# Zero-padded low parts of q, masks as planned units, and casts that the planner may give to ScalarE or VectorE, in a hybrid SSD and attention layer

## The chip, the core and the metric

The kernel runs as one program on one core of a Trainium2 chip. The metric is the device time of one execution in microseconds (us). The kernel before ran three times: 936.17, 939.4 and 940.26 us, median 939.4. One more execution was profiled; it took 935.09 us, and the profile's span, from its first to its last instruction, is 933.4 us.

## The reference

A decoder layer on 512 tokens of width 1024, in float32. In short:

```
h1  = rms_norm(x) * (1 + scale1) + shift1            # scale, shift, gate from silu(c) @ w_ada
z, xbc, dt, q, k, v = split(h1 @ w_in)
y_ssd = group_norm( (SSD scan of xbc, 16 heads, 4 chunks of 128) * silu(z) )
q, k  = rms_norm per head of 64 (q also / 8)
for (window, dilation) in (128,1), (512,4), (2048,16):
    softmax attention over t, t-d, t-2d, ...; the three are merged by their softmax denominators
y_att = rms_norm(merged)
x = x + gate1 * (concat(y_ssd, y_att) @ w_out)
x = x + gate2 * (square(relu(h2 @ w_ff1)) @ w_ff2)    # h2: a second modulated rms_norm
```

The three dilated windows are computed as one causal softmax whose scores get an additive mask: 0, log 2 or log 3 where one, two or three windows hold the key, and -1e30 where none does.

## The kernel before, in words

Activations lie transposed, with channels on the 128 partitions and the 512 tokens along the free dimension. Each float32 operand of a product is split into a high part (a cast to the type fp32r) and a low part (the operand less that cast). A dense product is three matmuls, high by high, high by low and low by high (`mm3`, lines 149 to 152). A weight tile (128 x 1024) comes by DMA into `wraw`, ScalarE casts the high part `whi`, GpSimd or VectorE subtracts the low part `wlo`, and 24 matmuls of 128 x 512 use it.

The stages in order of time: norm 1 and the first projections (to about 90 us); the convolution channels (`conv`, lines 560 to 586), each with one ScalarE and three VectorE passes (line 568) out of the PSUM bank; then a long region in which a planner decides the order (to about 560 us); then the last part of the output projection, norm 2 and the MLP to the end, in which dense products follow one another.

Just before the region, in iteration `n == 8` of the loop at line 945, `make_masks()` (lines 406 to 441) is called. It builds the attention mask and four small selection matrices (`selm`, `gsum`, `selT`, `gsel`) and clears `rhl`, with iota and affine selects on GpSimd and everything else on VectorE.

The region holds the z, q, k and v projections (the jobs of line 182, eight tiles of z, then four batches of q, k and v), the SSD scan of 16 heads, the gated norm, the attention of 16 heads in eight pairs, and most of the output projection. Each step is a unit: an engine, a cost in ns, the function that issues it, what it needs and makes, the buffers that it takes and gives back, and a due time (`unit`, line 1022). `place_units` (lines 1025 to 1089) goes through them by list scheduling: on each engine the unit that can start first, with a slack in favour of the one due earlier; the engine with the earliest start issues next. It assumes the written costs, and VectorE free from 8000 ns on. The order found is the program order of every engine and of the DMA queue on SyncE (SP); at run time each engine works in that order and waits at semaphores.

In the SSD scan each head needs VectorE for a product with the decay (line 676), for a low part of 128 x 1280 (line 684) and for two additions of a result (lines 694 and 696). Attention may open only when all 16 heads are summed (`att_open`, line 1279), as it reuses their memory.

For each q or k tile a square is taken on ScalarE, its high part is cast on VectorE (`sq_hi`, line 742), its low part is subtracted on GpSimd (`sq_lo`), and two matmuls sum rows (lines 1188 and 1189). The four gated-norm groups go the same way.

For the scores of a pair of heads, `st_dma` stacks tiles: QA holds the high part of q of the even head twice, once on each half of the partitions; KA holds the high part of k of that head above and its low part below; QB and KB serve the odd head. One matmul of 128 rows then gives high by high plus high by low. The low part of q, made by GpSimd for both heads in one tile `ql` of which there are two (`st_lo`, lines 797 to 802), needs only the high part of k, so its matmul uses 64 rows:

```
nc.tensor.matmul(p[:, o:o + w], lhsT=ql[r, s], rhs=Ks[r, :w], start=False, stop=True)
```

Each head has four such couples, of 512, 384, 128 and 256 columns (lines 843 to 850). Then VectorE adds the mask and takes the maximum (line 859), ScalarE exponentiates (`soft`), VectorE divides by the sums in four passes (`att_norm`, lines 872 to 877), TensorE transposes (line 887), ScalarE and VectorE make high and low parts (lines 894 and 900), and eight matmuls weigh v (`weighted_sum`, line 623; the SSD heads use it too).

The second half of the modulation vector is computed by 32 steps on VectorE (`ada_step`, line 1004, helper line 278) that read tiles by DMA.

Of the kernel before, what the change touches and what calls it, by code (L numbers as in the profile page):

```python
# [10 lines left out]
F32 = mybir.dt.float32  # L11
# [6 lines left out]
P = 128  # L18
T = 512
# [25 lines left out]
def tile_hybrid_layer(ctx, tc, xT, vec, c_row, ada_e, ada_r, w_a, w_dt, w_x, w_z, w_v, w_qk,  # L45
# [60 lines left out]
    nc.vector.memset(one_f, 1.0)  # L106
    one_r = constp.tile([P, P], F32R, name="one_r")
# [298 lines left out]
    def make_masks():  # L406
        di, dj = ftile().bitcast(I32), ftile().bitcast(I32)
        wc, we = ftile(), ftile()
        nc.gpsimd.iota(di, pattern=[[-1, T]], base=T - P, channel_multiplier=1)
        nc.vector.memset(wc, 1.0)  # L410
        nc.gpsimd.affine_select(wc, wc, pattern=[[1, T]], base=2 * P - T, channel_multiplier=-1,
                                compare_op=OP.is_ge, fill=0.0)
        for m in (3, 15):
            nc.vector.tensor_scalar(dj, di, m, None, op0=OP.bitwise_and)
            nc.vector.tensor_copy(we, dj)
            nc.vector.tensor_scalar(we, we, 0.0, None, op0=OP.is_equal)
            nc.vector.tensor_add(wc, wc, we)
        nc.gpsimd.affine_select(wc, wc, pattern=[[-1, T]], base=T - P, channel_multiplier=1,
                                compare_op=OP.is_ge, fill=0.0)
# [4 lines left out]
        sf, sg = ftile(), ftile()  # L424
        nc.vector.memset(sf, 1.0)
        nc.gpsimd.affine_select(sf[:8], sf[:8], pattern=[[-2, 4], [-1, 2], [0, 64]], base=0,
                                channel_multiplier=1, compare_op=OP.is_equal, fill=0.0)
        nc.vector.memset(sg, 0.0)
        nc.vector.memset(sg[:12, :4], 1.0)
        nc.gpsimd.affine_select(sg[:12, :4], sg[:12, :4], pattern=[[-1, 4]], base=-8,  # L430
                                channel_multiplier=1, compare_op=OP.is_equal, fill=0.0)
        nc.vector.memset(sg[:64, 22:23], 1.0)
        nc.vector.memset(sg[64:, 23:24], 1.0)
        nc.vector.memset(sg[:, 187:188], 0.25)
        nc.vector.tensor_copy(selm, sg[:, 16:P + 22])
        nc.vector.tensor_copy(gsum, sg[:, 176:P + 179])
        nc.vector.tensor_copy(rhl, sg[:, T - 1:].to_broadcast([P, T]))
        for d, r in ((selT, sf[:8]), (gsel, sg[:12, :4])):
            nc.vector.tensor_copy(d, sg[:, T - 1:].to_broadcast([P, d.shape[1]]))
            nc.vector.tensor_copy(d[:r.shape[0]], r)  # L440
            nc.vector.tensor_copy(d[32:32 + r.shape[0]], r)
# [297 lines left out]
    def sq_hi(g):  # L739

        S["sh", g] = gp.tile([P, T], F32R, tag="sh", name="sh", bufs=1)
        nc.vector.tensor_copy(S["sh", g], S["sq", g])  # L742
# [54 lines left out]
    def st_lo(pair, i):  # L797
        t = S["lo", i] = S["qp"].tile([P, T], F32R, tag="qk"[i] + "l", name="qk"[i] + "l", bufs=2 - i)
        nc.gpsimd.tensor_tensor(t, raws[pair // 2, 2 * (pair % 2) + i], f(S["hi", i]),
                                op=OP.subtract)  # L800
        if i == 0:
            stacks[pair].append(t)
# [33 lines left out]
    def att_scores(h, n, p):  # L836

        QA, QB, KA, KB, ql = stacks[h // 2]
        Qs, Ks = (QA, KA) if h % 2 == 0 else (QB, KB)
        r = slice(h % 2 * 64, h % 2 * 64 + 64)  # L840
        S["sp", h, n] = p
        for i, o in QBANK[n]:
            for lo in range(2):
                s, w = slice(i * P, (i + 1) * P), (i + 1) * P
                if lo:
                    nc.tensor.matmul(p[:, o:o + w], lhsT=ql[r, s], rhs=Ks[r, :w], start=False,  # L846
# [25 lines left out]
    def att_norm(h):  # L872
        A, st = S["soft", h]
        nc.vector.reciprocal(st[:, 12:16], st[:, 8:12])
        for i in (3, 2, 0, 1):
            a = A[:, QOFF[i]:QOFF[i] + (i + 1) * P]
# [68 lines left out]
    for n, c in enumerate(XBC_REST):  # L945
# [11 lines left out]
        if n == 8:  # L957
            sum_cols(arow)
            make_masks()
# [47 lines left out]
    def ada_end():  # L1007
# [10 lines left out]
                 cb=3, st=2, ql=2, qh=1, kh=1, kl=1, vhl=2, z8=8, o=1)  # L1018
# [5 lines left out]

    def place_units():


        free = dict(PE=0.0, DVE=8000.0, ACT=1000.0, POOL=0.0, SP=0.0)
# [11 lines left out]
        while left:  # L1040
            best = {}
            for u in left:
                eng, cost, fn, needs, makes, take, give, due, lands = u
                start = free[eng]
                ok = True
                for n in needs:
                    if n not in made:
                        ok = False
                        break
                    t, e = made[n]  # L1050
                    if e != eng:
                        t += LEAD.get(eng, 0)
                    start = max(start, t)
                if not ok:
                    continue
                for r, _ in take:
# [9 lines left out]
                if b is None or start < b[0] - SLACK.get(eng, 0):  # L1066
                    best[eng] = (start, u)
            assert best, [(u[0], u[4], u[3], [n for n in u[3] if n not in made]) for u in left[:12]]
            eng = min(best, key=lambda e: best[e][0])
            start, u = best[eng]  # L1070
            left.remove(u)
# [52 lines left out]
    for j, job in enumerate(JOBS):  # L1124
# [37 lines left out]
        else:  # L1162
# [6 lines left out]
            unit("DVE", 430, lambda g=g: sq_hi(g), [("sq", g), ("open", b)], ("sh", g), [("sh", g)], due=t + 1.5)  # L1169
# [21 lines left out]
    for b in range(4):  # L1191
        t = (13, 17, 23, 27)[b]

        for n, g in enumerate(rows_of[b]):
            unit("PE", 460, lambda b=b, g=g: rows_sum(b, g), [("sh", g), ("sl", g), ("open", b)],
# [5 lines left out]
        needs = [("power", b)]  # L1201
# [14 lines left out]
    for c in range(8):  # L1216
# [8 lines left out]
        unit("DVE", 900, lambda c=c: pair_lo(c), [("ph", c)], ("xdt", c), give=[("f2", k)], due=t)  # L1225
# [9 lines left out]
    for h in range(16):  # L1235
# [5 lines left out]
        unit("DVE", 1750, lambda h=h: wt_mul(h), needs, ("mul", h),  # L1241
             give=[("cb", h // 4)] if h % 4 == 3 else [], due=h + 0.3)
        unit("ACT", 1270, lambda h=h: wt_hi(h), [("mul", h)], ("hi", h), [("H", ("s", h))], due=h + 0.4)
        unit("DVE", 1750, lambda h=h: wt_lo(h), [("hi", h)], ("lo", h), [("L", ("s", h))],
# [5 lines left out]
             due=h + 0.8)  # L1250

# [5 lines left out]
    for g in range(4):  # L1257
# [9 lines left out]
        unit("DVE", 430, lambda k=k: sq_hi(k), [("gs", g), ("open", GATE_ROWS[g])], ("sh", k), [("sh", k)], due=t + 2)  # L1267
# [11 lines left out]
    def att_open():  # L1279
        ssd.close()  # L1280
        S["qp"] = att.enter_context(tc.tile_pool(name="qp", bufs=2))
        S["ssq"] = S["qp"].tile([P, T], F32, name="ssq_a", bufs=1)

    unit("PE", 0, att_open, [("so", h) for h in range(16)] + [("mul", 15)], "att", due=15)

# [5 lines left out]
    for n in range(ADA):  # L1291
        t = 15 + n * 0.42
# [3 lines left out]
        unit("DVE", 760, lambda n=n: ada_step(n), [("al", n), ("ac", n % 2)], ("as", n),  # L1296
# [5 lines left out]
    for p in range(8):  # L1302
# [4 lines left out]
        unit("POOL", 1430, lambda p=p: st_lo(p, 1), [("kh", p)], ("kl", p), [("kl", p)],  # L1307
             [("raw", ("q", b, i + 1))], due=t)
        unit("ACT", 640, lambda p=p: st_hi(p, 0), [("sc", p, 0), ("kh", p)], ("qh", p), [("qh", p)], due=t)
        unit("POOL", 1430, lambda p=p: st_lo(p, 0), [("qh", p)], ("ql", p), [("ql", p)],  # L1310
             [("raw", ("q", b, i))], due=t)
# [12 lines left out]
    for a in range(16):  # L1324
# [3 lines left out]
        for n in range(3):  # L1328
            k = ("sp", a, n)
            unit("PE", (440, 480, 260)[n], lambda a=a, n=n: att_scores(a, n, xbank(("sp", a, n))),  # L1330
                 [("sk", p), ("sq", p), ("ql", p)] + ([("sp", a, n - 1)] if n else []), k, [("x", k)],
                 [("st", p), ("ql", p)] if e and n == 2 else [], due=t)
            unit("DVE", (690, 850, 420)[n], lambda a=a, n=n: att_max(a, n),
                 [k] + ([("mx", a, n - 1)] if n else []), ("mx", a, n), [A] if n == 0 else [],
# [3 lines left out]
        unit("DVE", 1400, lambda a=a: att_norm(a), [("soft", a)], ("norm", a), due=t + 0.4)  # L1338
        for n in range(3):
            k = ("fl", a, n)  # L1340
            unit("PE", (460, 460, 230)[n], lambda a=a, n=n: att_flip(a, n, xbank(("fl", a, n))), [("norm", a)], k, [("x", k)],
# [29 lines left out]
    for c in range(8):  # L1371
# [3 lines left out]
        needs += [("kl", 7), ("ql", 7)] if c < 3 else [("vp", 7)] if c < 5 else [("mx", 15, 0)]  # L1375
# [202 lines left out]
```

## Time and profile before

| quantity | value |
|---|---|
| median of three runs | 939.4 us |
| profiled execution, and its span | 935.09 us, 933.4 us |
| TensorE busy (modelled) | 876.9 us, 94% of the span |
| VectorE busy | 622.3 us, 67% |
| ScalarE busy | 416.2 us, 45% |
| GpSimd busy | 277.9 us, 30% |
| mean granted TensorE clock | 0.974 |

The span is cut into windows and groups in the text. PE is TensorE's matmul, PEld its weight load, DVE VectorE, ACT ScalarE, POOL GpSimd, SP the queue that issues DMAs. A matmul's shown duration runs past the start of the next one, since matmuls are pipelined: what a matmul costs is read from start to start. A note in brackets at the end of a timeline row is idle time of that engine before the instruction, and who ended it. "PEclk" is the granted clock of TensorE, 1.00 being full speed.

### The profile page before, as it was taken

How to read it: one execution, taken by the hardware profiler on the slowest of the kernel's cores; microseconds unless marked ns; L12 is line 12 of the kernel's file. 1: busy time of each engine (PE TensorE's matmuls, PEld its weight loads, DVE VectorE, ACT ScalarE, POOL GpSimd, SP SyncE). 2: the span in 40 equal slices, each digit the busy share in tenths (PEclk: the TensorE clock that was granted, in tenths of full speed). 3: DMA queues.
4: the chain of work that ended last, by engine and by line, in shares of the span. 5: the costliest groups of instructions: out<-in, count | busy, mean ns of one | idle time of the engine just before them, and what ended most of it. 6: DMA issues, size and time to landing. Idle time of an engine off the chain costs nothing.

```text
span 933.4 us, 11344 instructions
## 1 busy us (share of the span) xinstructions
PE 876.9 (94%) x4112; PEld 717.6 (77%) x4112; DVE 622.3 (67%) x1047; ACT 416.2 (45%) x721; POOL 277.9 (30%) x172
## 2 busy tenths in 40 slices
PE   4988896999879999999999998999999999999998
PEld 4756784877657777777777888988888888888887
DVE  7989976798999699895957578774422333442331
ACT  4225432868554475574854544434312123432210
POOL 3313344586757755365352322000000000000000
PEclk9999997999989999998998999999999999999999
DMA  8743352444532835243271232453232223223320
GB/s 331 241 156 124 105 201 92 168 156 147 194 113 102 251 93 166 80 124 87 87 223 45 68 124 72 154 189 118 90 108 96 91 97 107 91 91 119 118 101 24
DMA packets 43111, 120.01 MB, mean 129 GB/s; under 512 B 5264, under 2 KB 5792, under 8 KB 43056
## 3 DMA queue, kind: packets, MB, share of 16 engines
q1 hardware_dynamic: 43056, 119.29, 39.1%
q8 instruction: 32, 0.52, 0.2%
q14 instruction: 23, 0.19, 0.1%
HBM read 108.70 MB, written 2.18 MB: 119 GB/s over the span
## 4 chain that ended last, share of the span: by engine, by line
PE 66%; DVE 24%; DMA 4%; issue 3%; ACT 2%; POOL 1%; SPq 0%; POOLq 0%; DVEq 0%; ACTq 0%
PE ps L150 19%; PE ps L152 19%; PE ps L151 19%; DVE wa L278 3%; DVE wk_L L684 3%; DVE ada L278 2%; PE ps L623 2%; PE ps L846 2%; DMA ada<-in_ada_r_dram 2%; PE ps L849 2%; DVE f L568 1%; PE ps L887 1%; DVE wk_A L676 1%; DMA wk_A<-arow_d 1%; DVE sh L742 1%
## 5 line engine op out<-in xcount | busy, mean ns | idle before, releaser
L112 ACT CAST whi<-wraw 128x1024 fp32r<-128x1024 f32 (+1 forms) x84 | 86.3, 1030 | 247.6 <-PE ps L151 220.3
L150 PE MATMUL ps<-hh,whi 128*128 128x512 f32 (+1 forms) x390 | 159.4, 412 | 14.7 <-DVE f L568 12.3
L115 DVE TENSOR_TENSOR wlo<-wraw,whi 128x1024 fp32r<-128x1024 f32 x66 | 80.7, 1223 | 136.4 <-ACT whi L112 134.9
L151 PE MATMUL ps<-hl,whi 128*128 128x512 f32 (+1 forms) x390 | 155.4, 398 | 2.2 <-DVE hl L125 2.2
L152 PE MATMUL ps<-hh,wlo 128*128 128x512 f32 (+1 forms) x390 | 155.2, 398 | 0.0
L1115 POOL TENSOR_TENSOR wlo<-wraw,whi 128x1024 fp32r<-128x1024 f32 x40 | 105.8, 2649 | 105.3 <-ACT whi L1111 85.5
L151 PE MATMUL ps<-ul,whi 128*128 128x512 f32 (+1 forms) x272 | 102.4, 377 | 0.0
L150 PE MATMUL ps<-uh,whi 128*128 128x512 f32 (+1 forms) x272 | 102.4, 377 | 0.0
L152 PE MATMUL ps<-uh,wlo 128*128 128x512 f32 (+1 forms) x272 | 102.4, 377 | 0.0
L150 PEld LDWEIGHTS ps<-hh,whi 128*128 128x128 f32 x390 | 76.3, 197 | 33.7 <-issue 14.7
L151 PEld LDWEIGHTS ps<-hl,whi 128*128 128x128 f32 x390 | 76.9, 197 | 17.6 <-DVE hl L125 3.5
L152 PEld LDWEIGHTS ps<-hh,wlo 128*128 128x128 f32 x390 | 76.4, 196 | 16.4
L151 PE MATMUL ps<-h2l,whi 128*128 128x512 f32 x224 | 87.2, 389 | 0.0
L150 PE MATMUL ps<-h2h,whi 128*128 128x512 f32 x224 | 87.1, 389 | 0.0
L152 PE MATMUL ps<-h2h,wlo 128*128 128x512 f32 x224 | 87.1, 389 | 0.0
L278 DVE CUSTOM_DVE_ANT_0 ada<-ada 128x512 f32<-128x512 f32 x64 | 57.7, 911 | 22.6 <-DMA ada<-in_ada_r_dram 22.6
L115 POOL TENSOR_TENSOR wlo<-wraw,whi 128x1024 fp32r<-128x1024 f32 (+1 forms) x18 | 41.5, 2307 | 91.7 <-ACT whi L112 91.7
L150 PEld LDWEIGHTS ps<-uh,whi 128*128 128x128 f32 x272 | 51.2, 188 | 9.5
L152 PEld LDWEIGHTS ps<-uh,wlo 128*128 128x128 f32 x272 | 51.2, 188 | 9.3
L151 PEld LDWEIGHTS ps<-ul,whi 128*128 128x128 f32 x272 | 51.2, 188 | 9.3
L1494 DVE SCALAR_TENSOR_TENSOR x<-ps,modc,x 128x512 f32<-128x512 f32 (+1 forms) x17 | 12.2, 719 | 60.6 <-PE ps L152 60.6
L1111 ACT CAST whi<-wraw 128x1024 fp32r<-128x1024 f32 x40 | 42.0, 1051 | 22.3 <-PE ps L151 11.9
(286 smaller groups left out, 1801.5 us busy)
## 6 DMA issues: line engine op xcount, KB each, us to landing
wraw<-in_w_f_dram SPq DMA_DIRECT2D x60, 512.0 KB, 3.3
ada<-in_ada_r_dram SPq DMA_DIRECT2D x64, 256.0 KB, 3.2
wk_A<-arow_d SPq DMA_DIRECT2D x16, 640.0 KB, 5.1
wa<-in_ada_e_dram SPq DMA_DIRECT2D x16, 512.0 KB, 6.7
wraw<-in_w_qk_dram SPq DMA_DIRECT2D x16, 512.0 KB, 4.2
wraw<-in_w_o_dram SPq DMA_DIRECT2D x16, 512.0 KB, 3.4
wraw<-in_w_x_dram SPq DMA_DIRECT2D x10, 512.0 KB, 3.4
wraw<-in_w_z_dram SPq DMA_DIRECT2D x8, 512.0 KB, 4.3
```

What stands on the lines that cost most here:

```text
L112: a = nc.scalar.copy(hi, src)
L115: return a, (leng or nc.vector).tensor_tensor(lo, src, f(hi), op=OP.subtract)
L150: pinned(nc.tensor.matmul(dst, lhsT=lh, rhs=rh, start=start, stop=False), pin)
L151: nc.tensor.matmul(dst, lhsT=lh, rhs=rl, start=False, stop=False)
L152: nc.tensor.matmul(dst, lhsT=ll, rhs=rh, start=False, stop=stop)
L278: return nc.vector.tensor_tensor_reduce(out=w, in0=w, in1=c, scale=1.0, scalar=0.0, op0=OP.mult, op1=OP.add, accum_out=dst)
L623: nc.tensor.matmul(p[:, j * P:], lhsT=t[:, m:m + P], rhs=W[i][:, OFF[j]:OFF[j] + BLK[j]], start=n == 0, stop=n == 7)
L684: nc.vector.tensor_tensor(S["L", h], dec[h], f(S["H", h]), op=OP.subtract)
L846: nc.tensor.matmul(p[:, o:o + w], lhsT=ql[r, s], rhs=Ks[r, :w], start=False, stop=True)
L849: nc.tensor.matmul(p[:, o:o + w], lhsT=Qs[:, s], rhs=Ks[:, :w], start=True, stop=False)
L1111: nc.scalar.copy(S["w", j][0], S["wraw", j])
L1115: nc.gpsimd.tensor_tensor(lo, S.pop(("wraw", j)), f(hi), op=OP.subtract)
```

## The change

It makes these edits. (1) The low parts of q go to two tiles of 128 rows, one for each head of a pair; the 64 rows of the other head are set to zero once, and the low matmul takes all 128 rows of the stacked k. There is one such tile for each head of the pair, where there were two buffers for both. The low part is made in two operations of 64 rows, each on GpSimd or VectorE. The DMAs that stack q now come after the second of them. (2) `make_masks` becomes units of the region: memsets go to GpSimd, the copies into the selection matrices to ScalarE, the arithmetic of the mask stays on VectorE. (3) The cast of squares may go to ScalarE or VectorE. (4) The softmax division becomes a reciprocal on VectorE and four units that may go to ScalarE or VectorE. For a unit with two engines the planner takes the engine on which it would end first. (5) Planner numbers: VectorE is free from 2000 ns on instead of 8000, the costs of four kinds of VectorE unit rise, and the modulation steps are due three units earlier.

```diff
+    zeros = constp.tile([P, 1], F32, name="zeros")
+    nc.vector.memset(zeros, 0.0)
...
-    def make_masks():
...
+    def mask_0():
+        a, b, wc, S["we"] = [rawp.tile([P, T], F32, tag="vt", name="mk", bufs=4) for _ in range(4)]
+        S["di"], S["dj"], S["wc"] = a.bitcast(I32), b.bitcast(I32), wc
+        nc.gpsimd.iota(S["di"], pattern=[[-1, T]], base=T - P, channel_multiplier=1)
+        nc.gpsimd.memset(wc, 1.0)
...
+    def mask_1(m):
+        dj, wc, we = S["dj"], S["wc"], S["we"]
+        nc.vector.tensor_scalar(dj, S["di"], m, None, op0=OP.bitwise_and)
+        nc.vector.tensor_copy(we, dj)
+        nc.vector.tensor_scalar(we, we, 0.0, None, op0=OP.is_equal)
+        nc.vector.tensor_add(wc, wc, we)
...
+    def mask_3():
+        wc, we = S["wc"], S["we"]
         nc.vector.tensor_scalar(mask, wc, 0.0, NEG, op0=OP.is_equal, op1=OP.mult)
         for n in (2, 3):
             nc.vector.tensor_scalar(we, wc, float(n), math.log(n), op0=OP.is_equal, op1=OP.mult)
             nc.vector.tensor_add(mask, mask, we)
...
+    def sel_1():
+        sg = S["sg"]
+        nc.scalar.copy(selm, sg[:, 16:P + 22])
+        nc.scalar.copy(gsum, sg[:, 176:P + 179])
...
-    def sq_hi(g):
+    def sq_hi(g, eng):
...
-        nc.vector.tensor_copy(S["sh", g], S["sq", g])
+        (eng.copy if eng is nc.scalar else eng.tensor_copy)(S["sh", g], S["sq", g])
...
+    def st_qlo(pair, e, eng):
+        r = slice(e * 64, e * 64 + 64)
+        eng.tensor_tensor(S["qz", e][r], raws[pair // 2, 2 * (pair % 2)][r], f(S["hi", 0][r]),
+                          op=OP.subtract)
...
-                    nc.tensor.matmul(p[:, o:o + w], lhsT=ql[r, s], rhs=Ks[r, :w], start=False,
+                    nc.tensor.matmul(p[:, o:o + w], lhsT=ql[:, s], rhs=Ks[:, :w], start=False,
                                      stop=True)
...
+    def att_norm(h, i, eng):
+        A, st = S["soft", h]
+        a = A[:, QOFF[i]:QOFF[i] + (i + 1) * P]
+        if eng is nc.scalar:
+            nc.scalar.activation(a, a, AF.Copy, scale=st[:, 12 + i:13 + i])
+        else:
             nc.vector.tensor_scalar(a, a, st[:, 12 + i:13 + i], None, op0=OP.mult)
...
-            make_masks()
...
-                 cb=3, st=2, ql=2, qh=1, kh=1, kl=1, vhl=2, z8=8, o=1)
+                 cb=3, st=2, ql0=1, ql1=1, qh=1, kh=1, kl=1, vhl=2, z8=8, o=1)
...
-        free = dict(PE=0.0, DVE=8000.0, ACT=1000.0, POOL=0.0, SP=0.0)
+        free = dict(PE=0.0, DVE=2000.0, ACT=1000.0, POOL=0.0, SP=0.0)
...
+                if "/" in eng:
+                    i = min((0, 1), key=lambda i: begin(eng.split("/")[i]) + cost[i])
+                    eng, cost = eng.split("/")[i], cost[i]
...
+            unit("ACT/DVE", (620, 950), lambda eng, g=g: sq_hi(g, eng), [("sq", g), ("open", b)], ("sh", g), [("sh", g)], due=t + 1.5)
...
+    k = [("vt", ("mask", n)) for n in range(4)]
+    unit("POOL", 2300, mask_0, [], "mask0", k, due=4)
+    for m in (3, 15):
+        unit("DVE", 2100, lambda m=m: mask_1(m), ["mask0" if m == 3 else ("mask1", 3)], ("mask1", m), due=7)
+    unit("POOL", 900, mask_2, [("mask1", 15)], "mask2", due=7)
+    unit("DVE", 2800, mask_3, ["mask2"], "mask", give=k, due=7.5)
+    k = [("f2", ("sel", n)) for n in range(2)]
+    unit("POOL", 3200, sel_0, [], "sel0", k, due=0)
+    unit("ACT", 600, sel_1, ["sel0"], "sel1", due=1)
+    unit("ACT", 2600, sel_2, ["sel1"], "sel2", give=k, due=1.5)
...
+    def qz_zero(e):
+        r = slice(64 - e * 64, 128 - e * 64)
+        nc.gpsimd.tensor_copy(S["qz", e][r], zeros[r].to_broadcast([64, T]))
...
-        t = 15 + n * 0.42
+        t = 12 + n * 0.42
...
+        for e in range(2):
+            unit("POOL/DVE", (1430, 690), lambda eng, p=p, e=e: st_qlo(p, e, eng),
+                 [("qh", p), ("qz", e)] + ([("ql", p, 0)] if e else []), ("ql", p, e),
+                 [("ql%d" % e, p)], [("raw", ("q", b, i))] if e else [], due=t)
...
-        unit("SP", 2300, lambda p=p: st_dma(p, 0), [("qh", p), ("sk", p)], ("sq", p), give=[("qh", p)],
+        unit("SP", 2300, lambda p=p: st_dma(p, 0), [("qh", p), ("sk", p), ("ql", p, 1)], ("sq", p), give=[("qh", p)],
...
+        unit("DVE", 170, lambda a=a: att_inv(a), [("soft", a)], ("inv", a), due=t + 0.4)
+        for i in range(4):
+            unit("ACT/DVE", ((370, 320), (480, 430), (600, 540), (730, 650))[i],
+                 lambda eng, a=a, i=i: att_norm(a, i, eng), [("inv", a)], ("norm", a, i), due=t + 0.4)
```

More of the change, by code (lines that the diff above doesn't have):

```diff
@@ L1023, in unit @@
         units.append((eng, cost, fn, tuple(needs), makes, tuple(take), tuple(give), due, lands))
+    engines = dict(DVE=nc.vector, ACT=nc.scalar, POOL=nc.gpsimd)
     def place_units():
-        free = dict(PE=0.0, DVE=8000.0, ACT=1000.0, POOL=0.0, SP=0.0)
+        free = dict(PE=0.0, DVE=2000.0, ACT=1000.0, POOL=0.0, SP=0.0)
         made = {}
@@ L1043, in place_units, with begin @@
                 eng, cost, fn, needs, makes, take, give, due, lands = u
[L1044 to L1054, printed above, removed]
-                    continue
+                if any(n not in made for n in needs):
+                    continue
+                def begin(e):
+                    return max([free[e]] + [made[n][0] + (LEAD[e] if made[n][1] != e else 0)
+                                            for n in needs])
+                if "/" in eng:
+                    i = min((0, 1), key=lambda i: begin(eng.split("/")[i]) + cost[i])
+                    eng, cost = eng.split("/")[i], cost[i]
+                    fn = lambda fn=fn, e=eng: fn(engines[e])
+                    u_ = (eng, cost, fn) + u[3:]
+                else:
+                    u_ = u
+                start = begin(eng)
                 for r, _ in take:
@@ L1224, in tile_hybrid_layer @@
         unit("ACT", 640, lambda c=c: pair_hi(c), [("pd", c)], ("ph", c), [("xd", c)], due=t)
-        unit("DVE", 900, lambda c=c: pair_lo(c), [("ph", c)], ("xdt", c), give=[("f2", k)], due=t)
+        unit("DVE", 1150, lambda c=c: pair_lo(c), [("ph", c)], ("xdt", c), give=[("f2", k)], due=t)
     for n in range(3):
@@ L1266, in tile_hybrid_layer @@
              due=t + 1)
-        unit("DVE", 430, lambda k=k: sq_hi(k), [("gs", g), ("open", GATE_ROWS[g])], ("sh", k), [("sh", k)], due=t + 2)
+        unit("ACT/DVE", (620, 950), lambda eng, k=k: sq_hi(k, eng), [("gs", g), ("open", GATE_ROWS[g])], ("sh", k), [("sh", k)], due=t + 2)
         unit("POOL", 1430, lambda k=k: sq_lo(k), [("sh", k)], ("sl", k), [("sl", k)], [("f2", (k, 0))],
@@ L1282, in att_open @@
         S["ssq"] = S["qp"].tile([P, T], F32, name="ssq_a", bufs=1)
+        for e in range(2):
+            S["qz", e] = S["qp"].tile([P, T], F32R, name=f"qz{e}", bufs=1)
+    def qz_zero(e):
+        r = slice(64 - e * 64, 128 - e * 64)
+        nc.gpsimd.tensor_copy(S["qz", e][r], zeros[r].to_broadcast([64, T]))
     unit("PE", 0, att_open, [("so", h) for h in range(16)] + [("mul", 15)], "att", due=15)
+    for e in range(2):
+        unit("POOL", 600, lambda e=e: qz_zero(e), ["att"], ("qz", e), due=15)
     ADA = 32
@@ L1295, in tile_hybrid_layer @@
              due=t - 0.6, lands=3200)
-        unit("DVE", 760, lambda n=n: ada_step(n), [("al", n), ("ac", n % 2)], ("as", n),
+        unit("DVE", 850, lambda n=n: ada_step(n), [("al", n), ("ac", n % 2)], ("as", n),
              give=([("z8", ("ac", n % 2)), ("z8", ("aw", n % 2))] if n > 29 else []), due=t)
```

88 lines of the change are left out of this document (37 added, 51 removed).

## The prediction

> **What bounds the kernel now.** I read the page first, then the waits of TensorE (PE), then windows over the planned region, then timelines of the places where PE loses time.
>
> ```profile
> PE 876.9 (94%) x4112; PEld 717.6 (77%) x4112; DVE 622.3 (67%) x1047; ACT 416.2 (45%) x721; POOL 277.9 (30%) x172
> PEclk9999997999989999998998999999999999999999
> ```
>
> PE is the bound: 94% of the span, and nobody else is near. So a microsecond counts if PE spends it idle, at a lowered clock, or on slow matmuls. The clock is below nine tenths in five slices. Who made PE wait (total, times, longest):
>
> ```profile
> PE ps L150 <- DVE f L568: 12.3, 3, 7.6
> PE ps L782 <- DVE rhl L115: 6.6, 1, 6.6
> PE ps L623 <- DVE wk_L L684: 4.8, 5, 1.5
> ```
>
> The longest single wait is on the last convolution (L568). The windows answer gives, for each stretch, its length, busy time of PE, PEld, DVE, ACT and POOL with counts, the granted clock and DMA:
>
> ```profile
> 154.90:159.40 4.50, 4.48 (x11) 3.57 (x12) 1.45 (x2) 3.48 (x5) 2.89 (x2) 0.50 0.00 0
> 319.80:323.20 3.40, 3.40 (x9) 2.33 (x8) 3.37 (x11) 0.52 (x1) 2.39 (x2) 0.52 1.05 243
> 425.60:432.40 6.80, 6.80 (x19) 5.24 (x19) 4.76 (x17) 3.59 (x14) 2.50 (x2) 0.51 0.45 151
> 493.90:500.70 6.80, 6.80 (x20) 5.19 (x21) 5.12 (x17) 1.20 (x3) 0.00 (x0) 0.51 0.22 77
> 302.00:420.00 118.00, 115.63 (x534) 88.07 (x533) 102.19 (x236) 72.96 (x166) 67.93 (x41) 0.99 0.49 143
> 420.00:560.00 140.00, 140.00 (x654) 111.45 (x653) 95.68 (x212) 77.27 (x163) 51.80 (x29) 0.95 0.34 106
> 180.00:300.00 120.00, 106.11 (x486) 86.72 (x484) 113.98 (x100) 77.45 (x123) 88.22 (x55) 0.96 0.44 148
> ```
>
> Two regimes. From 180 to 300, the SSD scan, VectorE is busy 114.0 of 120 and PE only 106.1: VectorE sets the pace, and attention cannot open before the scan's last head. From 302 on PE is busy 255.6 of 258 and VectorE has room: there PE's own speed sets the pace. The first four rows are stretches at half clock.
>
> **Edit 1, the scores.** Starts of one head's eight score matmuls, with the dense matmuls before them, from the timeline of PE:
>
> ```profile
> 420.62 0.39 PE L151 MATMUL ps<-hl,whi 128*128 128x512 f32 x1
> 420.84 0.39 PE L152 MATMUL ps<-hh,wlo 128*128 128x512 f32 x1
> 421.07 0.39 PE L849 MATMUL ps<-st 128*128 128x512 f32 x1
> 421.39 0.50 PE L846 MATMUL ps<-st,ql 64*128 64x512 f32 x1
> 421.82 0.44 PE L849 MATMUL ps<-st 128*128 128x384 f32 x1
> ...
> 423.38 0.38 PE L846 MATMUL ps<-st,ql 64*128 64x256 f32 x1
> 423.69 0.50 PE L849 MATMUL ps<-st 128*128 128x512 f32 x1
> ```
>
> Dense matmuls of 512 columns start 0.22 to 0.23 us apart. The high score matmul of 512 columns takes 0.32 to its successor, the low one of 64 rows 0.43. The head takes 423.69 - 421.07 = 2.62 us. No row says that PE waited for another engine. The weight loads (PEld) say where it goes:
>
> ```profile
> 420.62 0.19 PEld L152 LDWEIGHTS ps<-hh,wlo 128*128 128x128 f32 x1
> 421.39 0.18 PEld L846 LDWEIGHTS ps<-st,ql 64*128 64x128 f32 x1 [0.35 <-issue]
> ```
>
> A dense load starts with the matmul before its own, and is hidden. The load of the 64 rows starts only with its own matmul, after 0.35 us without a load. So each change between 128 and 64 rows breaks the overlap. Is it the change of height, or the shape of the work? The eight matmuls that weigh v have the same column counts, all with 128 rows and also two by two into one result:
>
> ```profile
> 469.92 0.39 PE L623 MATMUL ps<-wk_H,vhl 128*128 128x512 f32 x1
> ...
> 471.13 0.45 PE L150 MATMUL ps<-yh,whi 128*128 128x512 f32 x1
> ```
>
> From 469.92 to 471.13 is 1.21 us. With 128 rows throughout I expect the scores at this pace: (2.62 - 1.21) x 16 heads = 22.6 us less. All of it lies in 302 to 560, where PE is the bound. The ends are 0 (the loads stay exposed) and 22.6; I take 22.6, because L623 is the nearest row in all but the names.
>
> A rule speaks against it. The Trainium skill, TensorE: Matmul & The Clock Gate, Part 3, The mechanism, says that a weight load overlaps with matmuls in flight only when its row group differs. By it the padded loads, all of 128 rows, would be exposed and the scores keep today's time. The row at 420.62 disagrees: a load of 128 rows hidden behind a matmul of 128 rows.
>
> The half clock in attention goes with the scores, I think. The drops at 319.8, 425.6 and 493.9 come in or just after stretches of scores with gaps between loads; the one at 425.6 comes with PE shown as busy throughout. They last 3.4 + 6.8 + 6.8 = 17.0 us at 0.51 to 0.52, which loses about 8. Ends 0 and 8; I take 7, since the streams of L623 show no such drop.
>
> What the edit adds: the other half of each tile is cleared once, two GpSimd copies, hidden as GpSimd is busy 67.9 of 118 there. The low part becomes two operations of 64 rows, on GpSimd or VectorE:
>
> ```profile
> L799 POOL TENSOR_TENSOR ql<-raw,qh 128x512 fp32r<-128x512 f32 x8 | 10.9, 1363 | 0.1
> L115 DVE TENSOR_TENSOR ul<-f,uh 128x512 fp32r<-128x512 f32 x32 | 22.1, 692 | 0.9
> st<-qh SPq DMA_DIRECT2D x32, 128.0 KB, 2.8
> 420.90 2.42 SPq L810 DMA_DIRECT2D st<-qh  x4
> 374.27 0.38 PE L846 MATMUL ps<-st,ql 64*128 64x256 f32 x1
> 374.59 0.50 PE L849 MATMUL ps<-st 128*128 128x512 f32 x1
> ```
>
> The new wait: with one tile per head, the low part of the next pair waits until that head's scores are done, and the DMAs of q wait behind it. Queued behind are weight and modulation loads on SP, low parts of weights on GpSimd, and on PE whatever follows the next scores. The chain is 0.7 to 1.4 (low part, taking 64 rows at the price of 128) + 2.4 (issue) + 2.8 (landing) = 5.9 to 6.6 us. Today the next pair can follow after 0.3 us (374.27 to 374.59). Seven hand-overs, but the planner knows the chain and fills PE with dense matmuls: 0 to 7 x 6.3 = 44 us, and I take 3, half of one hand-over, since from 302 to 420 PE now idles only 2.4 us at seven eighths VectorE load.
>
> **Edit 2, the masks.** VectorE and PE before the region:
>
> ```profile
> 141.51 0.48 DVE L410 MEMSET f<- 128x512 f32 x1
> ...
> 153.24 1.53 DVE L568 SCALAR_TENSOR_TENSOR f<-ps,vecs,f 128x510 f32<-128x510 f32 x2
> ```
> ```profile
> 146.94 0.39 PE L152 MATMUL ps<-hh,wlo 128*128 128x512 f32 x1
> 154.92 0.77 PE L150 MATMUL ps<-hh,whi 128*128 128x512 f32 x1 [7.60 <-DVE f L568]
> ```
>
> The mask work starts at 141.51 and the last convolution ends behind it, at 154.8. PE stands 7.6 us for its bank and then runs 4.5 us at 0.50, losing 2.2 more. With the masks gone, three passes of about 0.74 from 141.5 end near 144, before PE asks at 147.3: 9.8 us saved, and nothing else is late there, since ScalarE's next casts of weights stand behind the same convolution.
>
> The mask arithmetic stays on VectorE, in a stage that VectorE bounds:
>
> ```profile
> L417 DVE TENSOR_TENSOR f<-f,f 128x512 f32<-128x512 f32 x2 | 1.4, 682 | 0.0
> L416 DVE TENSOR_SCALAR f<-f 128x512 f32<-128x512 f32 x2 | 0.8, 392 | 0.0
> DVE wk_A L676 <- ACT wk_A L85: 8.0, 1, 8.0
> L742 DVE CAST sh<-f 128x512 fp32r<-128x512 f32 x8 | 7.3, 912 | 2.2 <-ACT f L755 2.1
> L795 ACT CAST qh<-raw 128x512 fp32r<-128x512 f32 x8 | 5.0, 619 | 3.0 <-DMA st<-qh 3.0
> ```
>
> Thirteen operations of 392 to 682 ns: 5.1 to 8.9 us, about 7. It has a cover: VectorE stands 8.0 us once while the first exponentials are made. If the masks miss that gap, they lengthen the scan by 7. Memsets and selection copies go to GpSimd and ScalarE, which are not full in 180 to 300 (88 and 77 of 120).
>
> **Edits 3 to 5.** The eight casts of squares from 155 to 302 (L742, 7.3 us) go to ScalarE at about 619 ns each, as far as the planner finds it free. In the VectorE-bound scan that is worth 0 to 7.3; I take 3. Later casts and the divisions relieve VectorE where it is not the bound: nothing, as long as PE stays behind: its 118 us from 302 to 420 shrink by 1.41 for each of some eight heads, to about 107, and VectorE's 102 us shrink too. The new costs and due times reorder everything; of the waits at L782 and L623 I take neither gain nor loss.
>
> **The sum.** 22.6 + 7 + 9.8 + 3 - 3 = 39.4 us. Against the profiled execution of 935.1 that is 895.7. The median of the runs shown is 4.3 above the profiled one, so 900.0.
>
> **The rivals.**
> *Better order:* the waits at L782 (6.6) and L623 (4.8) also go, as VectorE's order has truer costs: 11.4 less, 888.6. For it: both waits are on VectorE in the scan. Against: the scan stays full.
> *The scan swallows the masks:* they miss the 8.0 us gap or the casts stay on VectorE, which the planner may choose, so that edit 3 does nothing, and attention opens as late as now. The 9.8 and the 3 are lost: 912.8. For it: VectorE at 95%.
> *Exposed loads:* full-height loads do not hide behind each other in the scores, the pace stays and with it the cold clock: 22.6 + 7 lost, 929.6. Against: the dense rows. The skill's rule named above would give this.
> *Slower:* the single tile for the low part makes PE stand at each hand-over between pairs. Without any hand-over cost the sum saves 39.4 + 3 = 42.4 us, so PE must stand 42.4 / 7 = 6.1 us at each of seven before the gain is gone, and 6.7 before it can be measured as a loss. The chain worked out above is 5.9 to 6.6; with its DMAs behind a weight load on SP, say 7: 939.4 - 42.4 + 49 = 946.0. For it: 374.27 to 374.59 shows one pair following another at once. Against: PE was fully busy from 420 to 560, so dense matmuls lay ready to be put between.
>
> **How the numbers follow.** Chances: forecast 0.63, with its own range 892 to 908; better order 0.12; scan 0.18; exposed loads 0.04; slower 0.03. The range 886 to 920 takes in the first three and their neighbours. A measurement of this kernel can tell about 0.5%, 4.7 us, from no change. Faster 0.95: the first four, less 0.02 for two of them together, which ends near 943; same 0.02; slower 0.03.
>
> **What would show it.** In the changed profile: L846's rows with 128 rows and a start-to-start of about 0.23 at 512 columns, a head's scores in about 1.2 us; no row of L150 waiting 7.6 us for L568; no clock below 0.9 after the scan; casts of squares in ScalarE's groups; the weighing of v unchanged. I am wrong if the padded matmuls still start 0.4 us apart, if PE's waits on VectorE from 180 to 300 grow past 14 us, or if rows of PE waiting for the DMAs of `st` or for `qz` add up to more than 10 us.

## The result, and the profile after

The changed kernel's median is 913.89 us (910.9 to 918.85), against 938.42 for the kernel before in the same comparison: a ratio of 0.9745, 95% interval 0.9694 to 0.9796. It is faster by 24.5 us where 39.4 were forecast. The time lies in the range (886 to 920) and above the forecast's own range (892 to 908). The profiled execution took 912.53 us, its span is 910.8. Ratios below are of executions at the usual clock: one execution of e12, at a granted clock of 0.563, took 1395.61 us and does not enter its ratio.

The page of the changed kernel, in the lines that were shown of before:

```profile
span 910.8 us, 11334 instructions
PE 851.4 (93%) x4112; PEld 709.8 (78%) x4112; DVE 624.2 (69%) x1017; ACT 436.6 (48%) x759; POOL 277.7 (30%) x177
PEclk9999999999999999999999999999999999999999
```

No slice of the clock stands below nine tenths any more, and PE is busy 25.5 us less. But a slice is 22.8 us long: within the slices the clock still stood at 0.50 for 3.4 us from 314.8 on, and again from 328.4 on.

VectorE is as busy as before (624.2 against 622.3), although casts and divisions were meant to leave it. 15 of the 20 casts and 12 of the 64 divisions did, but 12 of the 16 low parts of q came to it (11.7 us), and the same 64 operations of the modulation vector lasted 10 us longer (before first):

```profile
L278 DVE CUSTOM_DVE_ANT_0 ada<-ada 128x512 f32<-128x512 f32 x64 | 57.7, 911 | 22.6 <-DMA ada<-in_ada_r_dram 22.6
```
```profile
L280 DVE CUSTOM_DVE_ANT_0 ada<-ada 128x512 f32<-128x512 f32 x64 | 67.7, 1068 | 20.8 <-DMA ada<-in_ada_r_dram 20.6
```

The trace shows why one instruction can last so differently: some VectorE instructions stand while a GpSimd instruction runs, and the trace counts that as busy. Four divisions of 128x128 take 1.27 us at 323.65 (further below), with GpSimd idle. Here three take 2.75 us, and the first of them, 2.09 us long, ends 0.09 us after GpSimd's instruction:

```profile
445.07 2.39 POOL L1145 TENSOR_TENSOR wlo<-wraw,whi 128x1024 fp32r<-128x1024 f32 x1 [3.73 <-ACT whi L1141]
445.45 2.75 DVE L902 TENSOR_SCALAR wk_A<-wk_A,stat 128x128 f32<-128x128 f32 x3
```

With GpSimd idle, a VectorE instruction of one kind and shape on the same tiles varies by less than 0.05 us over all the runs. What instructions last beyond that (by more than 0.1 us) can be added up, as an estimate. During attention (the stretch defined below) it is 23 us of VectorE's busy time before and 30 in the changed kernel.

The scores of one head, from the timeline of PE, with the dense matmul behind them:

```profile
388.08 0.45 PE L869 MATMUL ps<-st 128*128 128x512 f32 x1
388.36 0.39 PE L866 MATMUL ps<-st,qz 128*128 128x512 f32 x1
388.59 0.34 PE L869 MATMUL ps<-st 128*128 128x384 f32 x1
...
389.28 0.28 PE L866 MATMUL ps<-st,qz 128*128 128x256 f32 x1
389.40 0.39 PE L152 MATMUL ps<-hh,whi 128*128 128x512 f32 x1
```

From 388.08 to 389.40 is 1.32 us, where the kernel before needed 2.62. The low matmul of 512 columns takes 0.23 us to its successor. And a weight load of 128 rows is hidden behind a matmul of 128 rows, as PEld shows three pairs earlier (the load of L869 at 310.17 starts with the matmul L866 at 310.17, for the matmul at 310.40):

```profile
310.17 0.19 PEld L869 LDWEIGHTS ps<-st 128*128 128x128 f32 x1
310.40 0.19 PEld L866 LDWEIGHTS ps<-st,qz 128*128 128x128 f32 x1
```

The wait for the last convolution before the region:

```profile
143.86 0.53 PE L152 MATMUL ps<-hh,whi 128*128 128x512 f32 x1 [1.98 <-DVE f L585]
```

The bracket says how long PE waited, and for whom. The 7.6 us that stood here are down to 2.0. (A wait of 3.1 us for an earlier convolution, near 85 us, is in both kernels.)

So where are the missing 15 us? These are the waits of PE from its first score to the last weighing of v, 309.94 to 506.40 (total, times, longest):

```profile
PE ps L799 <- DVE wk_L L925: 4.9, 1, 4.9
PE ps L869 <- DVE wk_L L925: 3.4, 3, 1.7
PE ps L869 <- DVE stat L879: 2.5, 2, 2.2
PE ps L869 <- DVE ya L941: 1.5, 1, 1.5
PE ps L640 <- DVE wk_L L925: 1.0, 2, 0.6
PE ps L912 <- DVE stat L879: 0.8, 1, 0.8
```

In the kernel before, the same stretch (315.92 to 527.57) had only 2.4 us of waits:

```profile
PE ps L887 <- DVE ya L916: 1.1, 1, 1.1
PE ps L782 <- DVE raw L787: 0.7, 2, 0.4
```

Scores (L869) and scale products (L799) now stand for VectorE, which has yet to do the low parts (L925) or the maxima (L879) of earlier heads. The longest such wait, with VectorE's timeline behind it:

```profile
323.65 1.27 DVE L902 TENSOR_SCALAR wk_A<-wk_A,stat 128x128 f32<-128x128 f32 x4
325.01 0.68 DVE L791 SCALAR_TENSOR_TENSOR f<-f,f 12x512 f32<-12x512 f32 x1
325.73 0.68 DVE L792 SCALAR_TENSOR_TENSOR f<-f,f 12x512 f32<-12x512 f32 x1
326.44 0.41 DVE L116 CAST rhl<-f 12x512 fp32r<-12x512 f32 x1
326.89 0.68 DVE L117 TENSOR_TENSOR rhl<-f,rhl 12x512 fp32r<-12x512 f32 x1
327.60 0.69 DVE L728 TENSOR_TENSOR f<-f,f 128x512 f32<-128x512 f32 x1
328.21 1.28 DVE L925 TENSOR_TENSOR wk_L<-ps,wk_H 128x512 fp32r<-128x512 f32 x2
```
```profile
328.95 0.80 PE L799 MATMUL ps<-rhl,selT 128*128 128x512 f32 x1 [4.94 <-DVE wk_L L925]
```

VectorE has no gap in these rows: divisions, then the row factors, a sum for the gated norm, and only then the low part that PE waits for. PE is not short of dense matmuls as such; it stands because its own next instruction is the one that waits.

The stretch as a whole, both kernels (length; busy of PE, PEld, VectorE, ScalarE, GpSimd; granted clock), before first:

```profile
315.92:527.57 211.65, 209.28 (x941) 159.74 (x940) 164.86 (x399) 129.87 (x296) 98.07 (x57) 0.96 0.39 117
```
```profile
309.94:506.40 196.46, 180.91 (x927) 150.46 (x927) 169.28 (x386) 139.30 (x315) 94.06 (x53) 0.98 0.42 123
```

PE's busy share fell from 99% to 92%, VectorE's rose from 78% to 86%. Split by time, the profiled spans differ by 22.6 us: the first score starts 6.0 us earlier, the stretch to the last weighing is 15.2 shorter, and from there to the first matmul of the MLP it is 47.2 before and 45.6 after.

For this stretch I take four numbers from each profile: the sum of the bracketed waits of PE, the clock's loss (half of the time that the trace shows at half clock), the sum of the score matmuls from start to start less waits, and the dense tiles of 24 matmuls in it.

| kernel | first score | length | waits | clock loss | scores | dense tiles |
|---|---|---|---|---|---|---|
| before | 315.9 | 211.6 | 2.4 | 8.5 | 43.5 | 19.5 |
| changed | 309.9 | 196.5 | 15.4 | 3.4 | 23.4 | 19.0 |
| e1 (64 rows, same order) | 309.1 | 210.7 | 6.0 | 8.2 | 44.5 | 19.0 |
| e7 (padding alone) | 319.6 | 205.6 | 20.6 | 6.8 | 22.8 | 19.3 |
| e8 (masks alone) | 305.3 | 220.1 | 10.3 | 10.2 | 43.1 | 19.5 |

Scores -20.1, clock -5.1, half a tile -2.7, waits +13.0: together -14.9, of the 15.2 us by which the stretch is shorter.

### The profile page after: what moved, and what is told of

Read it like the earlier page. It is cut to its first block, busy times and chain, and to the rows that moved or that the text cites. A ratio compares the mean times of both kernels' runs of the same rounds, so it can differ in the third digit from the quotient of the medians.

```text
span 910.8 us, 11334 instructions
## 1 busy us (share of the span) xinstructions
PE 851.4 (93%) x4112; PEld 709.8 (78%) x4112; DVE 624.2 (69%) x1017; ACT 436.6 (48%) x759; POOL 277.7 (30%) x177
## 4 chain that ended last, share of the span: by engine, by line
PE 65%; DVE 25%; DMA 3%; ACT 3%; issue 3%; POOL 0%; SPq 0%; DVEq 0%; POOLq 0%
PE ps L152 19%; PE ps L153 19%; PE ps L154 19%; PE ps L640 3%; DVE wa L280 3%; DVE ada L280 3%; DMA ada<-in_ada_r_dram 2%; DVE wk_L L701 2%; DVE wk_A L902 1%; DVE wk_A L879 1%; DVE wk_A L693 1%; DVE f L585 1%; ACT wk_A L85 1%; PE ps L912 1%; DVE raw L804 1%
## 5 line engine op out<-in xcount | busy, mean ns | idle before, releaser
L1145 POOL TENSOR_TENSOR wlo<-wraw,whi 128x1024 fp32r<-128x1024 f32 x40 | 108.6, 2720 | 73.5 <-ACT whi L1141 66.0
L280 DVE CUSTOM_DVE_ANT_0 ada<-ada 128x512 f32<-128x512 f32 x64 | 67.7, 1068 | 20.8 <-DMA ada<-in_ada_r_dram 20.6
L153 PEld LDWEIGHTS ps<-h2l,whi 128*128 128x128 f32 x224 | 42.1, 188 | 8.8
```

Source lines behind the costliest of these rows:

```text
L153: nc.tensor.matmul(dst, lhsT=lh, rhs=rl, start=False, stop=False)
L280: return nc.vector.tensor_tensor_reduce(out=w, in0=w, in1=c, scale=1.0, scalar=0.0, op0=OP.mult, op1=OP.add, accum_out=dst)
L1145: nc.gpsimd.tensor_tensor(lo, S.pop(("wraw", j)), f(hi), op=OP.subtract)
```

## The experiments

The theory at the start: the padding gives what was forecast on PE, and VectorE, with the order laid down for it, then holds PE back in attention. The rivals: the single tile for each low part (hand-over), or a pace that does not depend on the height of the tile. Each run is compared with the kernel before in its own comparison, so ratios are what to set beside each other.

**e1_low64.** Only the low matmul goes back to 64 rows. Every engine's instructions stand in the same order as in the changed kernel.

```diff
+        r = slice(h % 2 * 64, h % 2 * 64 + 64)
-                    nc.tensor.matmul(p[:, o:o + w], lhsT=ql[:, s], rhs=Ks[:, :w], start=False,
+                    nc.tensor.matmul(p[:, o:o + w], lhsT=ql[r, s], rhs=Ks[r, :w], start=False,
```

> The changed kernel in the same order of instructions on every engine, but the low part of q goes back to matmuls of 64 rows (the padded tiles are still made and cleared). Theory (the change of height between 128 and 64 rows breaks the overlap of weight loads, and the long slow stretches let the clock drop): a head's scores take 2.6 us instead of about 1.25, half clock comes back inside attention, and the time rises by 22.6 for the scores and up to 7 for the clock, less what hides in TensorE's 18 us of waits for VectorE there: 926 to 940 us. Rival (the pace of the scores does not depend on the height, and the gain of the change lies in the order): 910 to 918 us.

Measured: 926.83 us, ratio 0.985 (0.9818 to 0.9883), against 0.9745 for the changed kernel: about 10 us are lost. One head's scores in its timeline of PE:

```profile
348.51 0.39 PE L870 MATMUL ps<-st 128*128 128x512 f32 x1
348.83 0.49 PE L867 MATMUL ps<-st,qz 64*128 64x512 f32 x1
...
351.14 0.50 PE L1219 MATMUL ps<-sh,gsum 128*128 128x512 f32 x1
```

The pace is back at 2.63 us. Its waits in the stretch:

```profile
PE ps L799 <- DVE wk_L L926: 4.8, 1, 4.8
PE ps L870 <- DVE ya L942: 0.6, 1, 0.6
PE ps L640 <- DVE wk_L L926: 0.5, 1, 0.5
```

The height alone makes the pace, as the theory says. The rival that the gain lies in the order alone is out, although 1.5 of the 2.6% remain without the fast scores. The clock's loss is 8.2 against 3.4, but e5 below, in the same order and with fast scores, loses 6.8 too, so that this difference is not shown to be the height's. And in the same order the faster scores raise the waits from 6.0 to 15.4: of 21.1 us saved on the scores, 9.4 come back as waits, seen in one and the same program but for the height of 64 matmuls.

**e4_dma_first.** The DMAs of q no longer stand behind the second low part.

```diff
-[("qh", p), ("sk", p), ("ql", p, 1)], ("sq", p), give=[("qh", p)],
+[("qh", p), ("sk", p)], ("sq", p),
-[("raw", ("q", b, i))] if e else []
+[("raw", ("q", b, i)), ("qh", p)] if e else []
-[("sc", p, 0), ("kh", p)], ("qh", p)
+[("sc", p, 0), ("kh", p)] + ([("sq", p - 1)] if p else []), ("qh", p)
```

> The changed kernel with the DMAs of q's high part no longer planned behind its second low part (the high part's tile is given back by the low part instead), so that of the hand-over chain of 6 us only the low part remains after the scores of the pair before. Theory of VectorE's load: no change beyond that of another order, 910 to 918 us. Rival (the chain of low part and DMAs behind the single tile is what TensorE waits for): its waits from 300 to 560 fall by half and the time to 903 to 908 us.

Measured: 917.93 us, ratio 0.9751 (0.9718 to 0.9785), no difference from 0.9745; waits of 15.2 us in the stretch against 15.4. The order changed too, so this is not a clean removal, but the DMA part of the hand-over is not what PE waits for. Two tiles for each low part were not tried.

**e3_ql_pool.** All low parts of q on GpSimd.

```diff
-            unit("POOL/DVE", (1430, 690), lambda eng, p=p, e=e: st_qlo(p, e, eng),
+            unit("POOL", 1430, lambda p=p, e=e: st_qlo(p, e, nc.gpsimd),
```

> The changed kernel with all low parts of q on GpSimd (12 of the 16 are on VectorE in the changed kernel, 11.7 us there). Theory of VectorE's load: VectorE is relieved by 11.7 us between 300 and 470, TensorE's waits fall by a third, 907 to 911 us. Rival (hand-over chain): each low part takes 1.3 instead of 0.7 us in the chain, and GpSimd's queue stands behind the scores of the pair before; seven hand-overs of 0.6 us or more, 917 to 922 us.

Measured: 926.02 us, ratio 0.9849 (0.981 to 0.9887), slower than either side expected. VectorE was hardly relieved: the low parts left it, but its busy time in the stretch is 170.7 us against 169.3, as it now stands some 40 us for GpSimd instead of 30 (the estimate made above). So this run does not test what a lighter VectorE is worth. PE's largest wait from 302 to 545:

```profile
PE ps L152 <- ACT f L772: 10.2, 2, 7.4
```

A dense product waits for its bank, which ScalarE's copy and square of q or k must read. That the late low part, which holds the raw tile, stands behind it fits, but I argue it only.

**e2_div_act.** 42 of the 64 divisions on ScalarE, where the changed kernel has 12.

```diff
-            unit("ACT/DVE", ((370, 320), (480, 430), (600, 540), (730, 650))[i],
+            unit("ACT/DVE", ((370, 900), (480, 1000), (600, 1100), (730, 1200))[i],
```

> The changed kernel with VectorE's planned cost for the four softmax divisions raised (900 to 1200 ns), so that the planner gives 42 of the 64 to ScalarE instead of 12. Theory (VectorE's load sets the pace in attention, and gave back part of the scores' gain): some 30 divisions of about 0.5 us leave VectorE, TensorE's waits for VectorE from 300 to 560 fall from 18 us to about 10, and the time to 905 to 909 us. Rival (the hand-over of the single low-part tiles makes the waits): no change, 911 to 917. Second rival (ScalarE, now with divisions between exponentials, becomes the late one): 917 or more.

Measured: 926.49 us, ratio 0.9842 (0.9803 to 0.988). The time is the second rival's (917 or more). VectorE's load in the stretch fell to 161.5 us, and the waits rose to 24.4, most of them still for VectorE; the waits for ScalarE at L772 rose from 1.3 to 6.7 us (302 to 545). So a lighter VectorE alone does not bring fewer waits, once the order changes with it.

**e5_half_mod and e6_half_mod_before.** These two relieve VectorE without any change of order: the modulation steps of the region work on half their columns (half of that sum is left out), in the changed kernel and in the kernel before.

```diff
-        weigh(adac[:, 1 + n // 16, n % 16:n % 16 + 1], ada_t[2 + n % 2], ada_t[n % 2])
+        weigh(adac[:, 1 + n // 16, n % 16:n % 16 + 1], ada_t[2 + n % 2][:, :T // 2], ada_t[n % 2][:, :T // 2])
```

> The changed kernel with the 32 modulation steps of the planned region done over 256 of the 512 columns only (half of that sum is left out), at the same planned cost and so in the same order. VectorE loses about 0.4 us a step, 13 us in all, most of it between 230 and 430. Theory (VectorE's load in attention makes TensorE wait): waits from 302 to 545 fall from 17 us to 10 or 12 and the ratio to the kernel before from 0.9745 to 0.965 to 0.970. Rival (the waits come from chains of hand-overs, whatever VectorE's load): 0.972 to 0.977.

> The same edit in the kernel before (half of that sum is left out there too). Theory: TensorE sets the pace in its attention, so VectorE's relief is worth only what falls into the scan, nine steps: ratio 0.994 to 1.000. If VectorE's relief is worth as much here as in the changed kernel (0.985 to 0.993), the change did not move the bound in attention from TensorE to VectorE.

Measured: e5 908.76 us, ratio 0.9684 (0.966 to 0.9709); e6 933.27 us, ratio 0.9951 (0.9923 to 0.998). The relief is worth about 0.6% in the changed kernel and 0.5% before: both ratios fall into the theory's windows, but they cannot be told from each other, and for the changed kernel the intervals with and without the relief overlap (0.9694 to 0.9709). PE's waits in the stretch fell only from 15.4 to 13.5 us, not by the 5 to 7 that were expected. So VectorE's load did cost time before; in the changed kernel that is likely, but not clear of the noise. That the change moved the bound from TensorE to VectorE is not shown: the waits moved, the worth of VectorE's time hardly did.

**e7_pad_alone.** The kernel before with edit 1 alone (the padded tiles, their clearing and the low matmul of 128 rows as in the change).

```diff
+        for e in range(2):
+            unit(("POOL", "DVE")[e], (1430, 690)[e],
+                 lambda p=p, e=e: st_qlo(p, e, (nc.gpsimd, nc.vector)[e]), ...
```

> The kernel before with the zero-padded low parts alone (the low part of the even head on GpSimd, of the odd head on VectorE; masks, casts, divisions and the planner's other numbers as before). Theory (once the scores are fast, VectorE and the planned order hold TensorE back, with or without the other edits): 10 to 18 us faster, ratio 0.981 to 0.989. Rival (the waits in attention are made by the other edits, that is by the new order): the full 22.6 us and the clock, 25 to 30 us faster, ratio 0.968 to 0.974.

Measured: 934.33 us, ratio 0.9953 (0.9933 to 0.9973), about 4 us, below even the theory's window. The pace is there (scores 22.8 us in the stretch), and the waits rose from 2.4 to 20.6:

```profile
PE ps L784 <- DVE wk_L L906: 7.2, 2, 5.7
PE ps L855 <- DVE stat L865: 3.3, 1, 3.3
PE ps L893 <- DVE wk_A L883: 3.3, 2, 2.2
PE ps L152 <- DVE x L940: 2.0, 1, 2.0
```

None of them is a wait for the DMAs of q; one of 1.1 us ends with the first score. The rival that the other edits make the waits is out, though this kernel's order is its own, too.

**e8_masks_alone.** The kernel before with the masks as units, and VectorE planned as free from 2000 ns.

```diff
-            make_masks()
...
+    unit("POOL", 2300, mask_0, [], "mask0", k, due=4)
...
+    unit("DVE", 2800, mask_3, ["mask2"], "mask", give=k, due=7.5)
```

> The kernel before with the masks as units alone, and VectorE planned as free from 2000 ns. Theory: the wait of 7.6 us and the half clock behind it go, and with attention bound by TensorE the gain reaches the end: 6 to 10 us faster, ratio 0.989 to 0.994. Rival (the scan, bound by VectorE, takes the masks' 7 us and opens attention as late as now): 0.997 to 1.002.

Measured: 936.58 us, ratio 0.9983 (0.9964 to 1.0003). The number is the rival's, the mechanism is not: the first score starts 10.6 us earlier (305.3), so the scan did not swallow the masks. Attention then takes 8.5 us longer, with 7.9 more of waits and 1.7 more of clock loss:

```profile
PE ps L902 <- DVE ya L931: 4.6, 2, 3.1
PE ps L864 <- DVE stat L874: 3.1, 1, 3.1
```

**e9 to e12: the order.** Since padding and masks alone give 0.5 and 0.2%, and all edits but the padded matmul 1.5% (e1), I undid edits 3, 4 and 5 singly, and tried to mend the waits in the plan.

e9_casts_dve, the casts of squares on VectorE only:

```diff
-            unit("ACT/DVE", (620, 950), lambda eng, g=g: sq_hi(g, eng), ...
+            unit("DVE", 950, lambda g=g: sq_hi(g, nc.vector), ...
```

> The changed kernel with the casts of squares back on VectorE alone (15 of the 20 are on ScalarE in the changed kernel). Theory now (TensorE and VectorE hold each other in attention and in the scan; what TensorE saves turns into waits for VectorE unless VectorE is relieved): VectorE gets some 14 us back, most of it before 420, and the time rises by 6 to 14 us, ratio to the kernel before 0.981 to 0.990. Rival (the casts are not on the path): 0.972 to 0.977.

Measured: 925.05 us, ratio 0.9879 (0.9827 to 0.9931), within the theory's window, but VectorE's busy time rose by 7.3 us, not 14. The loss lies ahead of attention: the first score comes at 318.5, 8.6 us later than in the changed kernel, behind one wait of PE of 8.7 us for ScalarE (L772). That the casts cause this wait is not shown.

e10_div_dve, the divisions on VectorE only:

```diff
-            unit("ACT/DVE", ((370, 320), (480, 430), (600, 540), (730, 650))[i],
+            unit("DVE", (320, 430, 540, 650)[i],
```

> The changed kernel with all divisions on VectorE (12 of 64 are on ScalarE in the changed kernel, 7.7 us there). Theory now: VectorE gets 6 to 7 us back and gives up 3 to 5 us of time, ratio 0.977 to 0.980. Rival (a division on ScalarE stands in the way of its own successors there, as moving 30 more of them cost 8 us): as fast or faster, ratio 0.970 to 0.975.

Measured: 927.29 us, ratio 0.9891 (0.9855 to 0.9927), more than either side expected, with 25.4 us of waits in the stretch. VectorE is busy 16.7 us more there instead of 6 or 7; by the estimate, 14 us of that are standing for GpSimd.

e11_numbers, the planner's costs and due times as before:

```diff
-        t = 12 + n * 0.42
+        t = 15 + n * 0.42
-        unit("DVE", 2050, lambda h=h: wt_lo(h), ...
+        unit("DVE", 1750, lambda h=h: wt_lo(h), ...
```

> The changed kernel with the planner's costs and due times of four kinds of VectorE unit as before (low parts of pairs 900, decay product and low part 1750 and 1750, modulation steps 760 and due from 15). No instruction changes its work, only its place. If the order explains much of what edits 3 to 5 gave: ratio 0.980 to 0.990. If the relief of VectorE explains it: 0.972 to 0.978.

Measured: 923.61 us, ratio 0.9853 (0.9807 to 0.99). The work is as in the changed kernel, and the engines but for a few placements; the order costs about 1%.

e12_margin1500, banks that VectorE reads planned as free 1.5 us later:

```diff
-                    slots[r][rooms[r, key]] = end + SEEN[eng] + lands
+                    slots[r][rooms[r, key]] = end + SEEN[eng] + lands + (1500 if eng == "DVE" else 0)
```

> The changed kernel with the planner counting a PSUM bank that VectorE reads as free 1.5 us later than now, so that it puts other matmuls ahead of those that wait for VectorE. No instruction changes its work. Theory now (TensorE's 15 us of waits in attention come from VectorE being later than the plan has it): waits from the first scores to the last weighing fall below 10 us and the ratio to 0.966 to 0.971. Rival (the waits are a matter of VectorE's capacity and any order has them): 0.972 to 0.980.

Measured: 925.93 us, ratio 0.9867 (0.9816 to 0.9919), with 18.9 us of waits and 10.2 of clock loss in the stretch. The theory's expectation failed, and the time is above the rival's as well.

Five re-planned kernels (e2, e3, e9, e10, e12) take work from VectorE, give it some back, or only move it, and all five land at 0.984 to 0.989, as does e11; only e4 keeps 0.975. Undoing edits 3, 4 and 5 singly costs 1.1 to 1.5% each, more together than the three can have given. So these runs do not tell what casts, divisions or numbers are worth. They tell that the order the planner found in the changed kernel is about 1% better than six of its seven neighbours. None of the re-planned versions beats the changed kernel.

Two things differ between these orders in their traces. PE's waits for ScalarE at L772 (302 to 545) are 10.2 us in e3, 8.7 in e9 and e12 and 6.7 in e2, against 1.3 in the changed kernel. And VectorE stands for GpSimd some 35 to 44 us of the stretch in e3, e10, e11 and e12, against 30 in the changed kernel and 28 in e2 and e9 (estimates as above). Each slow order has at least one of the two. But e4, as fast as the changed kernel, has 4.4 us of the first as well, and no run changes either of them alone.

## Why the prediction was right or wrong

**The pace of the scores: right.** Forecast 22.6 us, measured 20.1 within the stretch; e1 shows that the height alone does it. The rule of the Trainium skill that was weighed (TensorE: Matmul & The Clock Gate, Part 3, The mechanism: loads overlap only when the row group differs) would have left the pace as it was; the rows at 310.17 and 388.08 decide against it here. The same section of the Trainium skill also lets a load into a background weight buffer run ahead, so the rows contradict that one line, not all that the section says. TensorEngine Tiling (Array Packing), Key Properties, also in the Trainium skill, says that changing the tiling mode drains the engine. If a matmul of 64 rows counts as another mode, e1 fits that; its price here is (44.5 - 23.4) / 128 score matmuls, 0.16 us each.

**The clock: 5.1 for 7, but not shown to come from the scores.** e5 and e7, both with fast scores, lose 6.8 us in the stretch, and e12, with fast scores as well, 10.2. Over the executions on record the mean clock was 0.967 to 0.978 in the kernel before and 0.979 to 0.988 in the changed one. It was 0.977 to 0.983 in e1 with slow scores, and 0.973 to 0.977 in e7 with fast ones. So the clock does not follow the scores alone. The page before shows four slices below nine tenths, where the prediction counts five; nothing in its sum hangs on that.

**The masks: right where they stood, wrong at the end.** The wait of 7.6 us is gone, and alone the edit opens attention 10.6 us earlier, near the 9.8 forecast. Yet alone it gives 0.2% at the end (e8). In the change the first score comes 6.0 us earlier, with 18 dense matmuls, 4.1 us, more done by then: 10.1 of the 12.8 for masks and casts.

**The step that failed** is in the first part: "there PE's own speed sets the pace" from 302 on, and with it the sentence that VectorE's later work costs nothing "as long as PE stays behind". PE's 255.6 busy of 258 us was read as a bound with VectorE's room (about a fifth) in reserve. But VectorE's 165 us in that stretch (some 23 of them standing for GpSimd) are chained head by head to PE and ScalarE in an order fixed in advance. When PE's part got shorter, PE ran into VectorE's, and 13.0 us of new waits came where the sum allowed 3; e1 shows 9.4 of them in one and the same order. I had put those 3 on the hand-over of the tiles; the waits are for VectorE, and e4 shows no worth in a shorter hand-over. The signs that I had named looked elsewhere and stayed silent: PE's waits on VectorE from 180 to 300 fell from 10.4 to 4.0 us, and no row of PE in the changed kernel waits for the DMAs of `st` or for `qz`. Waits for VectorE in attention were not among them.

**The rivals.** "The scan swallows the masks" gave 912.8 and the time is 913.9, but not for its reason: attention does open earlier, here and in e8, and the loss comes after. "Better order": the waits at L782 and L623 shrank, as PE's waits from 140 us to the first score fell from 23.8 to 12.6 us, of which 7.2 are the convolution's (9.2 to 2.0). How much of this reached the total is not known. "Exposed loads" and "slower by hand-over" did not happen.

**Luck.** That the time fell into the range is partly luck: with nearly the same edits in other orders, e2, e3, e9, e10, e11 and e12 took 923.6 to 927.3 us, all outside it.

**What stays open.** Why the orders differ by 1%: no run separates VectorE's load, its standing for GpSimd and the waits for ScalarE from each other, as every relief but e5 and e6 re-plans. Also open is how much casts and divisions give by themselves, and what sets the clock.

## What to carry to other kernels

A stretch in which an engine is busy 99% need not be bound by that engine alone: before a saving there is booked in full, ask how much shorter the stretch may get before the next engine in the chain (here VectorE at 78%) is late for the instruction at the head of a queue. Where a planner lays down the order, compare an edit with the order held fixed (e1, e5); a single undone edit that re-plans moved this kernel by 1% whatever it undid. And before work is moved off an engine because its busy share is high, see how much of that share is work: here some 14 to 17% of VectorE's busy time in attention was standing for GpSimd (estimate).

## What the runs showed of the hardware

A matmul of 64 rows between matmuls of 128 costs both of them: 2.63 us for a head's eight score matmuls (e1) against 1.32 with the rows filled up with zeros, which adds arithmetic and shortens the time. Half clock came also in a stretch without an idle row of PE (425.6 to 432.4 before); that the slow matmuls caused it is not shown.

Some VectorE instructions wait for a GpSimd instruction that is running, and the trace counts the wait as their duration: in the changed kernel a division of 128x128 took 0.29 us with GpSimd idle and up to 2.09 us beside it. In that kernel's attention 28 VectorE instructions lasted over 0.1 us longer than with GpSimd idle, and every one of them ended less than 0.6 us after a GpSimd instruction did.
